# The up products of two MLPs in pairs by Strassen's algorithm, the hidden tensor through DRAM

## The chip, the cores and the metric

The kernel runs on one core of a Trainium2 chip, in one launch. The metric is the device time of that core in microseconds, the median of several runs. TensorE (PE) multiplies, with its weight loads shown as PEld; VectorE (DVE), ScalarE (ACT) and GpSimd (POOL) do the elementwise work; SyncE (SP) issues nearly all DMAs. SBUF is the on-chip memory, PSUM the accumulators that matmuls write.

## The reference

A network of two layers over 16 + 1024 tokens of width 1024, in float32. Each layer adds a mixer (attention and a state space model in layer 0, a gated delta rule in layer 1) and an MLP to the residual, each between two norms. The change is in the MLP alone:

```
def sq_relu_mlp(h, w1, w2):
    return jnp.square(jax.nn.relu(h @ w1)) @ w2
...
hs = hs + rms_norm(sq_relu_mlp(hn, mlp_w1[i], mlp_w2[i]), post_mlp_norm[i])
```

`h` has up to 1040 rows (tokens) of 1024, `w1` is 1024 x 4096 and `w2` 4096 x 1024. In layer 1 the first 16 tokens are not needed any more, so its MLP works on 1024.

## The kernel before

Tokens lie along the free dimension, features in the 128 partitions. A tensor of 1024 features is eight tiles [128, 1040], numbered k; the hidden tensor of 4096 is 32 tiles, numbered m. Tokens go in chunks: `CH` = 352, 344, 344 in layer 0, `CH2` = 344, 344, 336 in layer 1, and `CH3` = 384, 384, 256 for the last product of layer 1.

Every product is made with split operands. A float32 value is held as `hi` (rounded to fp32r) and `lo` (the rest), and `unit` makes three matmuls for each k: hi by hi, hi by lo, lo by hi (lines 174 to 176 of the profile). `weight` makes the halves of a weight tile of [128, 1024]: SP loads `wraw` (two buffers), DVE casts it to `whi` (line 163), POOL subtracts to `wlo` (line 164). `whi` and `wlo` are rings of four tiles, so a cast waits until PE has done with the tile four before it. Each unit (one m, one chunk) goes to one PSUM bank, `mm` with three buffers; `tr` has three more and `ax` two.

`mlp` has two kinds of phases. `up([m])` makes hidden tile m: for each chunk 8 x 3 = 24 matmuls; then `ev` runs DVE (line 384: relu and the factor `rb`, 1/rms per token, from PSUM to a temporary), ACT (line 385: square), and `split`, that is ACT's cast to `hh` (line 226) and DVE's subtraction to `hl` (line 227). `down([a, b])` uses hidden tiles a and b: for each of eight output tiles and each chunk 2 x 3 = 6 matmuls, and DVE adds the bank to `acc` in SBUF (line 408); the first down copies with ACT instead. Group g is the down of hidden tiles 2g and 2g + 1. After four ups in one go the groups follow with two ups between each two of them, one by one, and then comes a last down of four tiles, which also starts the residual and the next norm. The hidden tiles stay in SBUF as `hh` and `hl`, in 33 slots of [128, 1040] that they share with `acc` and others.

The engines take their instructions in order. The Tile framework's scheduler sets each queue's order from its own costs, not from the text's order alone.

Of the kernel before, what the change touches and what calls it, by code (L numbers as in the profile page):

```python
# [1 line left out]

# [24 lines left out]
CH3 = ((16, 384), (400, 384), (784, 256))  # L27

# [20 lines left out]
class Net:  # L49
# [6 lines left out]
    def step(self, strand):  # L56
        """emit the next piece of a strand; whether there was one that need not wait"""
        self.busy, was = True, self.busy
        going = False
        while strand:  # L60
            try:
                going = next(strand[0]) is not WAIT
                break
            except StopIteration:
                strand.pop(0)
        self.busy = was
        return going

    def tick(self, n=1):
        """emit n more pieces of the work that runs beside the present one, of its strands in turn"""  # L70
# [24 lines left out]
    def until(self, name, strand=None):  # L95
        """emit of a strand, or of all, up to what is named"""
        while name not in self.done:
            if strand is None or not self.step(strand):
                self.clock += 0.5
                self.tick()  # L100
# [12 lines left out]
    def pause(self, us):  # L113
        """wait while the tensor engine is given work for some time"""
        t = self.clock + us
        while self.clock < t:
            yield WAIT
# [32 lines left out]
    def weight(self, src, n=1024, spare=False, fast=False):  # L150
        """a weight tile as hi + lo; spare: in slots, beside the weights in use"""
# [15 lines left out]
    def unit(self, pt, kts, wap, rhs, o, n):  # L167
        """One output tile [128, n]: three passes of split products over kts."""
# [25 lines left out]
    def rowscale(self, cols, n, nsub, invd):  # L194
        """cols(j): [128, sub] summands whose sum over partitions is wanted per token; returns
        1/sqrt(sum * invd + eps) in a PSUM tile [128, nsub * sub], the same in every partition."""
# [10 lines left out]
    def spread(self, r, sub, nsub):  # L207
        """[sub, nsub] per-token values to rows that every partition holds."""
# [13 lines left out]
    def split(self, hi, lo, src, gain=None, lo_eng=None):  # L222
        """hi + lo = src (* gain per partition) exactly."""
# [8 lines left out]
    def norm_in(self, st, m, c, chunks, hsn, gcol):  # L232
        """Account one piece of the residual stream for the next product: its square sum, and the
        piece times the norm's gain as hi + lo."""
# [21 lines left out]
    def pieces(self, src, c, chunks, eng, mid=None):  # L256
        """a chunk of a [128, 8, tokens] stream, some feature tiles to a slot"""
# [11 lines left out]
    def first_norm(self):  # L269
        """the first norm, of all but the first chunk in pieces beside the first product"""  # L270
# [29 lines left out]
    def residual(self, acc, ssq, reuse, gpost, hs_old, gpre, chunks):  # L300
        """hs + rms(acc) * gain, and what the next norm or the output takes of it. Returns a hook for
        the last product before it, which goes by chunks of tokens: a chunk is taken up while the next
        one is made. reuse gives its place to the next state."""
# [64 lines left out]

    def mlp(self, layer, st, hs_d, chunks, gpre, ahead=None):
        """gpre: the next norm's gain column, or None at the end."""  # L370
        nc = self.nc
        w1, w2 = self.io["w1"], self.io["w2"]
        hid = {}
        acc = None

        def up(ms, order):
            W = self.w_up if ms[0] == 0 else {m: self.weight(w1[layer, m]) for m in ms}

            def ev(m, c, pt):
                if m not in hid:  # L380
                    hid[m] = (self.slot("hh", F32R), self.slot("hl", F32R))
                o, n = chunks[c]
                t1, t2 = self.tmp("t1"), self.tmp("t2")
                nc.vector.scalar_tensor_tensor(t1[:, :n], pt, 0.0, st["rb"][:, o:o + n], op0=ALU.max, op1=ALU.mult)  # L384
                nc.scalar.activation(t2[:, :n], t1[:, :n], AF.Square)  # L385
                self.split(hid[m][0][:, o:o + n], hid[m][1][:, o:o + n], t2[:, :n])

            self.gemm(ms, range(8), lambda m, k: tuple(w[:, k * 128:(k + 1) * 128] for w in W[m]), lambda k: (st["hi"][k], st["lo"][k]), chunks, order, ev)

        def down(ks, last=False):  # L390
            first = ks[0] == 0
            W = {k: self.weight(w2[layer, k]) for k in ks}
            out, hook, ch = None, None, chunks
            if last:
                if ahead is None:
# [21 lines left out]
        up([0, 1, 2, 3], "c")  # L417
        acc = [self.slot("acc") for _ in range(8)]
        down([0, 1])
        up([4], "m")  # L420
        for g in range(1, 14):
            if g > 1:
                up([2 * g + 2], "m")
            down([2 * g, 2 * g + 1])
            up([2 * g + 3], "m")
        up([30], "m")
        up([31], "m")
        return down([28, 29, 30, 31], True)

# [20 lines left out]
    def s5_params(self):  # L450
# [24 lines left out]
        # powers 0..8 of exp(lambda dt), [128, 9, 16]  # L475
# [17 lines left out]
        # decay of a chunk and its rotation, as unit vectors 1, 2, 4 .. 128 chunks on  # L493
# [14 lines left out]
        # coef = (abar - 1) / lambda  # L508
# [15 lines left out]
        # bbar over b, -c_re and -c_im beside c  # L524
# [17 lines left out]
        # rotation tables over chunks, pairs 0..7 and 8..15  # L542
# [30 lines left out]
    def s5_mats(self, q):  # L573
        """Matrices of the groups 8 q .. 8 q + 7 for chunks of 8 tokens: inputs to state, inputs to
        outputs, and the state before the chunk to outputs."""
# [34 lines left out]
        # impulse response, then the Toeplitz matrices by reading it at shifted places  # L610
# [22 lines left out]
    def s5_ready(self, ud):  # L633
        """what the quarters need, back on chip, a quarter ahead"""
# [30 lines left out]
    def s5_quarter(self, q, ud):  # L665
# [21 lines left out]
        def rotate(dst, src, sign):  # L687
            """dst = src * exp(sign i phi)"""
# [59 lines left out]
    def glu(self):  # L748
        """gelu(y) * sigmoid(gelu(y) w + b), in place, with its square sum"""
# [34 lines left out]
    def normed(self, tiles, ssq, gcol, reuse=None):  # L784
        """rms norm over the features of 4 tiles, as hi + lo"""
# [11 lines left out]
    def attention(self, qd, kd, vd, vd0):  # L797
        """stick-breaking attention, by pairs of heads (a tile of features) and pairs of query tiles"""
# [12 lines left out]
        def load_v(p):  # L811
# [5 lines left out]
            # for a head and a block of keys, hi beside lo  # L817
# [10 lines left out]
        def weights(qk, h, i, kp=None, sg=None):  # L828
            """[q, keys] weights of q tile i"""
# [30 lines left out]
        def later(item, depth=DEP):  # L860
            """products wait for their operands behind the transposes of the next groups"""
# [4 lines left out]
        def outputs(p, pr, h, w, V, osb):  # L866
            # blocks of keys: (index, first q column, q columns)
# [87 lines left out]
    def mixer0(self, st, rows):  # L955
# [3 lines left out]
        # s5 inputs  # L959
# [22 lines left out]
        # token-wise scales for the products that have tokens in the partitions  # L982
# [7 lines left out]
        # values, tokens in the partitions  # L990
# [55 lines left out]
    def out_block(self, acc, w, ks, rhs, first, chunks, W=()):  # L1046
        """products of some feature tiles with the mixer's last weights"""
# [20 lines left out]
    def out_last(self, acc, W, ks, rhs, chunks, gpost, hs_d, gpre, ahead):  # L1068
        """the last of them, and the residual stream after it"""
# [19 lines left out]
    def token_col(self, pt, cols):  # L1089
        """cols(i): summands [128, tokens of tile i]; their sums per token, in column i of pt"""  # L1090
# [3 lines left out]
    def gates(self, st, rc):  # L1094
        """decays and write strengths of all heads, tokens in the partitions: [128, 9, 8]"""
# [74 lines left out]
    def take(self, t):  # L1170
        """weights of one tile of the input projection; loads those of the next one ahead"""
# [6 lines left out]
    def conv_in(self, st, tiles, order, hook=None):  # L1178
        """inputs of the causal convolution, for some tiles of 128 features"""
# [39 lines left out]
    def decays(self, Hs):  # L1219
        """decays between the tokens of a chunk, of all heads"""  # L1220
# [15 lines left out]
    def keys(self, h, xk, H):  # L1236
        """what the chunks of a head need of its keys, short of the state"""
# [66 lines left out]
    def queries(self, h, xq, H):  # L1304
        """what the chunks of a head need of its queries"""
# [34 lines left out]
    def solve(self, n, size, N, U, v):  # L1340
        """U = (I - N)^-1 of n strictly upper triangular blocks, a block in each partition"""
# [28 lines left out]
    def solve_first(self):  # L1370
        """the same for the first tokens of all heads"""
# [12 lines left out]
    def combine(self, H):  # L1384
        """inverses of the 128 x 128 blocks from those of their 32 x 32 blocks"""
# [51 lines left out]
    def values(self, h, x, H):  # L1437
        """values of a head, tokens in the partitions, times the keys' norms"""
# [560 lines left out]
```

## Time and profile before

| what | us |
|---|---|
| three runs | 3014.28, 3022.55, 3031.21 |
| median | 3022.55 |
| profiled execution: its span | 3011.3 |
| PE busy in it | 2838.4 (94%) |
| DVE, ACT, POOL busy in it | 1773.1, 892.8, 864.6 |
| MLP of layer 0, from about 738 to 1460 | 722 |
| MLP of layer 1, from about 2296 to 3000 | 704 |

For the profiled execution the span is the only time at hand. Its rows give a line of the kernel, an engine, an operation with its output and inputs, shapes, a count, the busy time, and the mean of one in ns; behind the second bar stand the engine's idle time ahead of these instructions and what ended it. A matmul's own duration is modelled and overlaps the next; what a matmul costs is read from start to start, or from the number of matmuls in a window.

### The profile page before, as it was taken

To read this page: it belongs to the slowest core of one execution; us is meant where nothing else is said; L and a number is where in the kernel's file an instruction comes from. 1 tells how busy PE (TensorE), PEld (TensorE's weight loads), DVE (VectorE), ACT (ScalarE), POOL (GpSimd) and SP (SyncE) were. 2 spreads that over 40 slices of the span, in tenths; PEclk is the share of its full clock that TensorE was granted. 3 is DMA by queue.
4 is the path that set the end of the run, shared out by engine and by line. 5 is a ranking of instruction groups with operands and counts; after the bars stand their busy time and mean duration, and the time that the engine had idled before them with its cause. 6 is when DMAs were issued, how large, how long until landed. Compare 5 with 4: busy or idle time off the path is not lost. (4 is left out here: it accounts for less than half of the span.)

```text
span 3011.3 us, 44561 instructions
## 1 busy us (share of the span) xinstructions
PE 2838.4 (94%) x17628; PEld 2685.8 (89%) x17628; DVE 1773.1 (59%) x3158; ACT 892.8 (30%) x1934; POOL 864.6 (29%) x628
## 2 busy tenths in 40 slices
PE   7899998999999999999896978999989999999998
PEld 7688667888999999999886978899988999999997
DVE  8633778667455555555646995545546455555555
ACT  4112566554311101111435423334434111111112
POOL 5551225225311221222522132211143222122123
PEclk9989567889999999999998999999999999999999
DMA  3435212134111111111426666453332111111113
GB/s 126 158 127 161 71 43 92 41 104 146 58 50 43 50 46 46 50 42 51 130 85 201 220 205 208 157 153 110 127 106 84 50 50 43 50 50 43 50 50 112
DMA packets 168289, 284.92 MB, mean 95 GB/s; under 512 B 40880, under 2 KB 108672, under 8 KB 168080
## 3 DMA queue, kind: packets, MB, share of 16 engines
q1 hardware_dynamic: 164192, 277.38, 28.8%
q10 hardware_dynamic: 3888, 4.69, 0.4%
q8 instruction: 139, 2.28, 0.3%
q14 instruction: 70, 0.57, 0.1%
HBM read 204.80 MB, written 77.21 MB: 94 GB/s over the span
## 5 line engine op out<-in xcount | busy, mean ns | idle before, releaser
L174 PE MATMUL mm<-ahi,whi 128*128 128x344 f32 (+2 forms) x2592 | 862.4, 333 | 33.5 <-DVE cx L1189 22.1
L164 POOL TENSOR_TENSOR wlo<-wraw,whi 128x1024 fp32r<-128x1024 f32 x181 | 439.5, 2430 | 1504.1 <-DVE whi L163 1138.1
L176 PE MATMUL mm<-ahi,wlo 128*128 128x344 f32 (+2 forms) x2592 | 844.9, 326 | 1.8 <-DVE wlo L164 1.8
L175 PE MATMUL mm<-hl,whi 128*128 128x344 f32 (+4 forms) x1920 | 619.1, 322 | 0.0
L174 PEld LDWEIGHTS mm<-ahi,whi 128*128 128x128 f32 x2592 | 497.2, 192 | 41.7 <-DVE cx L1189 23.3
L176 PEld LDWEIGHTS mm<-ahi,wlo 128*128 128x128 f32 x2592 | 497.0, 192 | 4.5 <-DVE wlo L164 2.9
L176 PE MATMUL mm<-hh,wlo 128*128 128x344 f32 (+4 forms) x1536 | 492.8, 321 | 2.9 <-POOL wlo L164 2.9
L408 DVE TENSOR_TENSOR acc<-mm,acc 128x344 f32<-128x344 f32 (+4 forms) x672 | 343.9, 515 | 253.4 <-PE mm L176 253.4
L174 PE MATMUL mm<-hh,whi 128*128 128x344 f32 (+4 forms) x1536 | 492.0, 320 | 0.1
L385 ACT ACTIVATE t<-t 128x344 f32<-128x344 f32 (+2 forms) x192 | 94.4, 492 | 1093.7 <-DVE t L384 1093.7
L175 PEld LDWEIGHTS mm<-hl,whi 128*128 128x128 f32 x1920 | 363.8, 189 | 1.3 <-issue 0.6
L175 PE MATMUL mm<-ml,whi 128*128 128x344 f32 (+2 forms) x1056 | 340.1, 322 | 0.7 <-DVE ml L227 0.7
L163 DVE CAST whi<-wraw 128x1024 fp32r<-128x1024 f32 x181 | 180.0, 997 | 196.7 <-PE mm L175 160.6
L176 PEld LDWEIGHTS mm<-hh,wlo 128*128 128x128 f32 x1536 | 289.2, 188 | 3.8 <-POOL wlo L164 3.5
L174 PEld LDWEIGHTS mm<-hh,whi 128*128 128x128 f32 x1536 | 289.5, 188 | 0.9 <-DVE acc L408 0.3
L227 DVE TENSOR_TENSOR hl<-t,hh 128x344 fp32r<-128x344 f32 (+2 forms) x192 | 162.2, 845 | 166.6 <-ACT hh L226 165.5
L175 PE MATMUL mm<-mh,whi 128*128 128x344 f32 (+2 forms) x768 | 246.8, 321 | 0.0
L175 PEld LDWEIGHTS mm<-ml,whi 128*128 128x128 f32 x1056 | 199.7, 189 | 1.1 <-DVE ml L227 1.0
L384 DVE SCALAR_TENSOR_TENSOR t<-mm,rb 128x344 f32<-128x344 f32 (+2 forms) x192 | 98.5, 513 | 121.0 <-PE mm L176 121.0
L175 PEld LDWEIGHTS mm<-mh,whi 128*128 128x128 f32 x768 | 144.6, 188 | 0.5 <-issue 0.2
L175 PE MATMUL mm<-hh,whi 128*128 128x344 f32 (+2 forms) x384 | 126.7, 330 | 0.0
L853 DVE TENSOR_TENSOR_SCAN keep<-keep,cst 128x400 f32<-128x400 f32 (+5 forms) x72 | 95.5, 1338 | 45.8 <-ACT keep L851 45.4
(425 smaller groups left out, 4530.0 us busy)
## 6 DMA issues: line engine op xcount, KB each, us to landing
wraw<-w SPq DMA_DIRECT2D x128, 512.0 KB, 3.5
wraw<-wino SPq DMA_DIRECT2D x32, 512.0 KB, 3.7
dm<-dmd SPq DMA_DIRECT2D x16, 520.0 KB, 4.8
hsd<-hs SPq DMA_DIRECT2D x48, 172.0 KB, 1.8
wraw<-wine SPq DMA_DIRECT2D x12, 512.0 KB, 3.7
wraw<-qkd SPq DMA_DIRECT2D x8, 520.0 KB, 3.6
acc<-acc SPq DMA_DIRECT2D x8, 520.0 KB, 4.6
dmd<-grow SPq DMA_DIRECT2D x8, 520.0 KB, 5.3
```

The lines of the kernel that those rows point to most:

```text
L163: nc.vector.tensor_copy(hi[:, :n], raw[:, :n])
L164: (nc.vector if fast else nc.gpsimd).tensor_sub(lo[:, :n], raw[:, :n], f(hi[:, :n]))
L174: nc.tensor.matmul(pt, wh, h[:, o:o + n], start=i == 0, stop=False)
L175: nc.tensor.matmul(pt, wh, l[:, o:o + n], start=False, stop=False)
L176: nc.tensor.matmul(pt, wl, h[:, o:o + n], start=False, stop=i == len(kts) - 1)
L227: (lo_eng or nc.vector).tensor_sub(lo, src, f(hi))
L384: nc.vector.scalar_tensor_tensor(t1[:, :n], pt, 0.0, st["rb"][:, o:o + n], op0=ALU.max, op1=ALU.mult)
L385: nc.scalar.activation(t2[:, :n], t1[:, :n], AF.Square)
L408: nc.vector.tensor_add(acc[m][:, o:o + n], pt, acc[m][:, o:o + n])
L853: v.tensor_tensor_scan(kp[:n, 0:L][:, ::-1], kp[:n, 0:L][:, ::-1], self.one_row[:n, :L], 1.0, op0=ALU.mult, op1=ALU.mult)
```

## The change

The order becomes: ups 0 to 5 as before, then 13 pairs of ups (m = 6 to 31), then 14 downs in a row, then the last down. A pair takes two weight tiles `ra` and `rb` (for m and m + 1) as blocks A11, A12 (k below 4, and from 4) and A21, A22, and the normed input as blocks B11, B12, B21, B22 by k and by token half (520 tokens in layer 0, 512 in layer 1). Strassen's algorithm in Winograd's form makes the four output blocks from seven products of blocks instead of eight, with sums of blocks ahead and behind:

- `halves_T`, once in each MLP, makes the sums of B blocks (T1 to T4) from the residual in DRAM times the norm's gains, and splits them: per layer 8 subtractions on DVE and 8 on POOL, 16 casts on ACT and 16 subtractions on DVE, of 520 or 512 columns, with 16 loads and 16 scalings.
- `ops` makes seven weight operands for each pair: four sums on POOL (`sS`), seven casts on ACT, seven subtractions on POOL, each of 512 columns. An operand takes half a tile of the `whi` and `wlo` rings.
- `product` makes 4 x 3 matmuls for each chunk: two chunks of 260 tokens in layer 0, one of 512 in layer 1. So a pair has 168 matmuls in layer 0 and 84 in layer 1. The banks go round over `mm`, `tr` and one `ax`, seven in all.
- Behind a pair's chunk stand one copy on ACT, seven sums on DVE (one input in PSUM), four `block`s on DVE (relu and `rb`, SBUF alone), and in `put` four squares on ACT and four stores to DRAM (`hd`).

Every hidden tile goes to DRAM, the first six too. `hidden` loads a tile back into a slot (`hr`) and splits it, an ACT cast and a DVE subtraction (line 229 of the changed kernel) of 1040 or 1024 columns. In layer 1 the 14 downs take two chunks of 512 (`CH4`) instead of three. Line numbers of `weight` and `ev` become 165, 166 and 552.

The diff, cut to `mlp` and what it uses; the rest of it removes comments only:

```diff
@@ -25,6 +26,7 @@
 CH3 = ((16, 384), (400, 384), (784, 256))
+CH4 = ((16, 512), (528, 512))
...
@@ -366,32 +368,174 @@
     def mlp_ahead(self, layer):
         self.w_up = {m: self.weight(self.io["w1"][layer, m], fast=FA >> m & 1) for m in range(4)}
+    def halves_T(self, st, hs_d, t0, h, gcol):
+        nc = self.nc
+        T = []
+        for j in range(4):
+            if j < 3:
+                p, q = self.slot("ta"), self.slot("tb")
+                parts = [p[:, :h], p[:, h:2 * h], q[:, :h], q[:, h:2 * h]]
+            else:
+                parts = [self.sp.tile([128, 520], F32, tag="sS", name="sS", bufs=4)[:, :h] for _ in range(4)]
+            for i, x in enumerate(parts):
+                k, o = j + i // 2 * 4, t0 + i % 2 * h
+                nc.sync.dma_start(x, hs_d[:, k, o:o + h])
+                nc.scalar.activation(x, x, AF.Copy, scale=self.gains[:, gcol + k:gcol + k + 1])
+            pl, pr, ql, qr = parts
+            nc.vector.tensor_sub(pl, pr, pl)
+            nc.gpsimd.tensor_sub(pr, qr, pr)
+            nc.vector.tensor_sub(qr, qr, pl)
+            nc.gpsimd.tensor_sub(ql, ql, qr)
+            out = []
+            for x in (parts[:2], parts[2:]):
+                hi, lo = self.slot("th", F32R), self.slot("tl", F32R)
+                for i in range(2):
+                    self.split(hi[:, i * h:i * h + h], lo[:, i * h:i * h + h], x[i])
+                out.append((hi, lo))
+            T.append(out)
+        return T
     def mlp(self, layer, st, hs_d, chunks, gpre, ahead=None):
         nc = self.nc
         w1, w2 = self.io["w1"], self.io["w2"]
+        hd = self.dr.tile([128, 32, NT], F32, tag="hd%d" % layer, name="hd", bufs=1)
         hid = {}
-        acc = None
+        t0, h = (0, 520) if layer == 0 else (16, 512)
+        half = ((0, 260), (260, 260)) if layer == 0 else ((0, 512),)
+        wide = chunks if layer == 0 else CH4
+        def put(m, o, n, x):
+            nc.scalar.activation(x[:, :n], x[:, :n], AF.Square)
+            nc.sync.dma_start(hd[:, m, o:o + n], x[:, :n])
         def up(ms, order):
             W = self.w_up if ms[0] == 0 else {m: self.weight(w1[layer, m]) for m in ms}
             def ev(m, c, pt):
-                if m not in hid:
-                    hid[m] = (self.slot("hh", F32R), self.slot("hl", F32R))
                 o, n = chunks[c]
-                t1, t2 = self.tmp("t1"), self.tmp("t2")
+                t1 = self.tmp("t1")
                 nc.vector.scalar_tensor_tensor(t1[:, :n], pt, 0.0, st["rb"][:, o:o + n], op0=ALU.max, op1=ALU.mult)
-                nc.scalar.activation(t2[:, :n], t1[:, :n], AF.Square)
-                self.split(hid[m][0][:, o:o + n], hid[m][1][:, o:o + n], t2[:, :n])
+                put(m, o, n, t1)
             self.gemm(ms, range(8), lambda m, k: tuple(w[:, k * 128:(k + 1) * 128] for w in W[m]), lambda k: (st["hi"][k], st["lo"][k]), chunks, order, ev)
+        room = []
+        bank = cycle((self.mm, self.tr, self.mm, self.tr, self.mm, self.tr, self.ax))
+        def operand(src, own=False):
+            if not room:
+                hi = self.sb.tile([128, 1024], F32R, tag="whi", name="whi", bufs=4)
+                lo = self.sb.tile([128, 1024], F32R, tag="wlo", name="wlo", bufs=4)
+                room.extend([(hi[:, :512], lo[:, :512]), (hi[:, 512:], lo[:, 512:])])
+            hi, lo = room.pop(0)
+            nc.scalar.copy(hi, src)
+            nc.gpsimd.tensor_sub(lo, src, f(hi))
+            return hi, lo
+        def ops(ma, mb):
+            ra, rb = self.raw(), self.raw()
+            nc.sync.dma_start(ra[:, :1024], w1[layer, ma])
+            nc.sync.dma_start(rb[:, :1024], w1[layer, mb])
+            a11, a12, a21, a22 = ra[:, :512], ra[:, 512:1024], rb[:, :512], rb[:, 512:1024]
+            S = [self.sp.tile([128, 520], F32, tag="sS", name="sS", bufs=4)[:, :512] for _ in range(4)]
+            o = [operand(a11)]
+            nc.gpsimd.tensor_add(S[0], a21, a22)
+            nc.gpsimd.tensor_sub(S[1], S[0], a11)
+            o.append(operand(S[1]))
+            o.append(operand(a12))
+            nc.gpsimd.tensor_sub(S[2], a11, a21)
+            o.append(operand(S[2]))
+            o.append(operand(a22))
+            o.append(operand(S[0]))
+            nc.gpsimd.tensor_sub(S[3], a12, S[1])
+            o.append(operand(S[3]))
+            return o
+        def pair(ma, mb, T):
+            A11, S2, A12, S3, A22, S1, S4 = ops(ma, mb)
+            B11 = lambda k: (st["hi"][k][:, t0:t0 + h], st["lo"][k][:, t0:t0 + h])
+            B21 = lambda k: (st["hi"][k + 4][:, t0:t0 + h], st["lo"][k + 4][:, t0:t0 + h])
+            B22 = lambda k: (st["hi"][k + 4][:, t0 + h:t0 + 2 * h], st["lo"][k + 4][:, t0 + h:t0 + 2 * h])
+            T1, T3 = (lambda k: tuple(x[:, :h] for x in T[k][0])), (lambda k: tuple(x[:, h:2 * h] for x in T[k][0]))
+            T4, T2 = (lambda k: tuple(x[:, :h] for x in T[k][1])), (lambda k: tuple(x[:, h:2 * h] for x in T[k][1]))
+            def product(A, B, then):
+                for c, (o, n) in enumerate(half):
+                    pt = next(bank)()[:, :n]
+                    for i in range(4):
+                        wh, wl = (w[:, i * 128:(i + 1) * 128] for w in A)
+                        bh, bl = B(i)
+                        nc.tensor.matmul(pt, wh, bh[:, o:o + n], start=i == 0, stop=False)
+                        nc.tensor.matmul(pt, wh, bl[:, o:o + n], start=False, stop=False)
+                        nc.tensor.matmul(pt, wl, bh[:, o:o + n], start=False, stop=i == 3)
+                    then(c, o, n, pt)
+            P, U, R, Q = {}, {}, {}, {}
+            def total(x, name, n, *ab):
+                x = self.tmp(name) if x is None else x
+                nc.vector.tensor_add(x[:, :n], *ab)
+                return x
+            def block(m, o, n, x):
+                nc.vector.scalar_tensor_tensor(x[:, :n], x[:, :n], 0.0, st["rb"][:, o:o + n], op0=ALU.max, op1=ALU.mult)
+                put(m, o, n, x)
+            def p1(c, o, n, pt):
+                P[c] = self.tmp("p1")
+                nc.scalar.copy(P[c][:, :n], pt)
+            def p2(c, o, n, pt):
+                block(ma, t0 + o, n, total(P[c], "", n, pt, P[c][:, :n]))
+            def p6(c, o, n, pt):
+                U[c] = total(None, "u2", n, pt, P[c][:, :n])
+            def p7(c, o, n, pt):
+                R[c] = total(None, "u3", n, pt, U[c][:, :n])
+            def p4(c, o, n, pt):
+                block(mb, t0 + o, n, total(None, "c21", n, pt, R[c][:, :n]))
+            def p5(c, o, n, pt):
+                Q[c] = total(U[c], "", n, pt, U[c][:, :n])
+                block(mb, t0 + h + o, n, total(R[c], "", n, pt, R[c][:, :n]))
+            def p3(c, o, n, pt):
+                block(ma, t0 + h + o, n, total(Q[c], "", n, pt, Q[c][:, :n]))
+            product(A11, B11, p1)
+            product(S2, T2, p6)
+            product(A12, B21, p2)
+            product(S3, T3, p7)
+            product(A22, T4, p4)
+            product(S1, T1, p5)
+            product(S4, B22, p3)
+        def hidden(k):
+            raw = self.slot("hr")
+            hi, lo = self.slot("hh", F32R), self.slot("hl", F32R)
+            nc.sync.dma_start(raw[:, t0:NT], hd[:, k, t0:NT])
+            self.split(hi[:, t0:NT], lo[:, t0:NT], raw[:, t0:NT])
+            hid[k] = (hi, lo)
         def down(ks, last=False):
             first = ks[0] == 0
+            for k in ks:
+                hidden(k)
             W = {k: self.weight(w2[layer, k]) for k in ks}
-            out, hook, ch = None, None, chunks
+            out, hook, ch = None, None, wide
             if last:
+                ch = chunks
                 if ahead is None:
                     ch = CH3
                 if ahead is not None:
@@ -415,19 +559,17 @@
             return out
         up([0, 1, 2, 3], "c")
+        T = self.halves_T(st, hs_d, t0, h, G_PREMLP + 8 * layer)
+        for m in range(4, UPC):
+            up([m], "m")
+        for m in range(UPC, 32, 2):
+            pair(m, m + 1, T)
         acc = [self.slot("acc") for _ in range(8)]
-        down([0, 1])
-        up([4], "m")
-        for g in range(1, 14):
-            if g > 1:
-                up([2 * g + 2], "m")
+        for g in range(14):
             down([2 * g, 2 * g + 1])
-            up([2 * g + 3], "m")
-        up([30], "m")
-        up([31], "m")
         return down([28, 29, 30, 31], True)
...
-NSLOT, NTMP, AHEAD = 33, 10, 4
+NSLOT, NTMP, AHEAD, UPC = 33, 10, 4, 6
...
-    st, hs = N.mlp(0, st, hs, CH, G_PREMIX + 8, N.mixer1_ahead)
+    with N.tc.tile_pool(name="m0", bufs=1) as N.sp:
+        st, hs = N.mlp(0, st, hs, CH, G_PREMIX + 8, N.mixer1_ahead)
...
-    N.mlp(1, st, hs, CH2, None)
+    with N.tc.tile_pool(name="m1", bufs=1) as N.sp:
+        N.mlp(1, st, hs, CH2, None)

```

How instructions move, first on DVE in layer 0, between two groups. `acc` is the accumulation, `whi` a weight tile's cast, `t` an up's evacuation, `hl` a hidden tile's subtraction. Before:

```order
L408 TENSOR_TENSOR acc<-mm,acc 128x352
L408 TENSOR_TENSOR acc<-mm,acc 128x344
L163 CAST whi<-wraw 128x1024
L408 TENSOR_TENSOR acc<-mm,acc 128x344
L163 CAST whi<-wraw 128x1024
L384 SCALAR_TENSOR_TENSOR t_9937<-mm,rb 128x352
L227 TENSOR_TENSOR hl<-t_9938,hh 128x352
```

Now:

```order
L165 CAST whi<-wraw 128x1024
L552 TENSOR_TENSOR acc<-mm,acc 128x344
L165 CAST whi<-wraw 128x1024
L552 TENSOR_TENSOR acc<-mm,acc 128x352
L229 TENSOR_TENSOR hl<-hr,hh 128x1040
L552 TENSOR_TENSOR acc<-mm,acc 128x344 x2
```

The two casts and a whole tile's `hl` subtraction now stand between the accumulations of one group and of the next, with no up behind them. This form stands at 8 of the 14 boundaries behind the downs of layer 0; at one there is an accumulation more ahead of `hl`, the last four have no `hl` left, and the first has both casts and then two `hl` in a row.

Then DVE in layer 1, at the same kind of place. Before:

```order
L408 TENSOR_TENSOR acc<-mm,acc 128x344 x2
L163 CAST whi<-wraw 128x1024
L408 TENSOR_TENSOR acc<-mm,acc 128x336
L163 CAST whi<-wraw 128x1024
L384 SCALAR_TENSOR_TENSOR t_26732<-mm,rb 128x344
L227 TENSOR_TENSOR hl<-t_26733,hh 128x344
```

Now:

```order
L552 TENSOR_TENSOR acc<-mm,acc 128x512 x9
L165 CAST whi<-wraw 128x1024 x2
L552 TENSOR_TENSOR acc<-mm,acc 128x512
L229 TENSOR_TENSOR hl<-hr,hh 128x1024
L552 TENSOR_TENSOR acc<-mm,acc 128x512 x6
```

Both casts now stand together, and `hl` follows one accumulation later; seven boundaries of layer 1 have this form.

Last POOL, which before had in these phases `L164 TENSOR_TENSOR wlo<-wraw,whi 128x1024` alone, one for each weight tile. Now, between two pairs of layer 0 (`sS` is a sum of weight blocks, `wlo` the low half of an operand):

```order
L438 TENSOR_TENSOR wlo<-wraw,whi 128x512
L449 TENSOR_TENSOR sS<-wraw 128x512
L450 TENSOR_TENSOR sS<-sS,wraw 128x512
L438 TENSOR_TENSOR wlo<-sS,whi 128x512
L453 TENSOR_TENSOR sS<-wraw 128x512
L438 TENSOR_TENSOR wlo<-sS,whi 128x512
L457 TENSOR_TENSOR sS<-wraw,sS 128x512
```

Sums and subtractions of 512 columns alternate on POOL, eleven of them for each pair.

More of the change, by code (lines that the diff above doesn't have):

```diff
@@ L1 @@
 import math
+from itertools import cycle
 import numpy as np
```

## The prediction

> **What bounds the kernel now.** I read the page first (busy shares, then the groups), then windows of the two MLPs, then the timeline around the places that the new order touches. The page's first rows:
>
> ```profile
> span 3011.3 us, 44561 instructions
> PE 2838.4 (94%) x17628; PEld 2685.8 (89%) x17628; DVE 1773.1 (59%) x3158; ACT 892.8 (30%) x1934; POOL 864.6 (29%) x628
> ```
>
> TensorE leads. Windows inside the MLP of layer 0 and of layer 1 (columns: sum, then PE, PEld, DVE, ACT, POOL, granted clock, DMA share, GB/s):
>
> ```profile
> 900.00:1000.00 100.00, 100.00 (x633) 100.00 (x632) 53.08 (x86) 13.71 (x29) 21.62 (x9) 1.00 0.15 48
> 2500.00:2600.00 100.00, 100.00 (x643) 100.00 (x642) 55.16 (x93) 11.62 (x24) 20.00 (x9) 1.00 0.14 43
> ```
>
> PE is never idle there, at full clock: a matmul costs 100/633 = 0.158 us in layer 0 and 100/643 = 0.1555 in layer 1. So fewer or cheaper matmuls pay in full, and every new PE wait costs in full.
>
> **Matmuls removed.** The pairs run at 260 and 512 columns. Prices by start to start: 256 columns (end of the last down of layer 1, first and last of 14), 512 columns (attention values, first and last of 14):
>
> ```profile
> 2984.36 0.28 PE L174 MATMUL mm<-hh,whi 128*128 128x256 f32 x1
> ...
> 2985.89 0.28 PE L175 MATMUL mm<-hl,whi 128*128 128x256 f32 x1
> ```
> ```profile
> 91.00 0.39 PE L1003 MATMUL mm<-wlo,ahi 128*16 128x512 f32 x1
> ...
> 94.01 0.40 PE L1004 MATMUL mm<-whi,alo 128*128 128x512 f32 x1
> ```
>
> 1.53/13 = 0.1177 us and 3.01/13 = 0.2315 us: 0.00044 us a column, so 0.1195 at 260 (estimate). Layer 0: 26 up products of 8 x 3 x 3 = 72 matmuls are 1872 x 0.158 = 295.8 us; 13 pairs of 7 x 2 x 12 = 168 are 2184 x 0.1195 = 261.0: -34.8. Layer 1: 1872 x 0.1555 = 291.1 against 13 x 84 = 1092 x 0.2315 = 252.8: -38.3. Layer 1's 14 downs go from 2016 matmuls (313.5 us) to 1344 of 512 (311.1): -2.4. Together **-75.5 us**.
>
> **The pairs' other work.** Rows for weights, sums and casts (groups; the POOL ones at 512 columns by form):
>
> ```profile
> L164 POOL TENSOR_TENSOR wlo<-wraw,whi 128x1024 fp32r<-128x1024 f32 x181 | 439.5, 2430 | 1504.1 <-DVE whi L163 1138.1
> L408 DVE TENSOR_TENSOR acc<-mm,acc 128x344 f32<-128x344 f32 (+4 forms) x672 | 343.9, 515 | 253.4 <-PE mm L176 253.4
> L163 DVE CAST whi<-wraw 128x1024 fp32r<-128x1024 f32 x181 | 180.0, 997 | 196.7 <-PE mm L175 160.6
> ```
> ```profile
> L591 POOL TENSOR_TENSOR s5mo<-s5mo,s5c 128x512 f32<-128x512 f32 x8 | 12.0, 1504 | 0.2
> L591 POOL TENSOR_TENSOR s5mi<-s5mi,s5c 128x512 f32<-128x512 f32 x8 | 10.1, 1282 | 0.1
> ```
>
> A pair gives PE 168 x 0.1195 = 20.1 us (layer 1: 84 x 0.2315 = 19.4). POOL gets 11 operations of 512: between 11 x 2.43/2 = 13.4 and 11 x 1.50 = 16.5. DVE gets 14 sums and 8 blocks of 260, at most 22 x 0.515 = 11.3; the blocks read SBUF alone and may hold POOL up (below), 8 x 0.5 = 4 at most. So POOL needs 13.4 to 20.5 of 20.1; I take 17.4 (middle row, 1.28 x 11 = 14.1, with 0.4 for a 260-wide block). Eight half tiles hold operands six products ahead (17 us), and seven PSUM banks absorb late sums. **Cost 0**, cover 2.0 to 2.7 us a pair. ACT's casts and squares lie ahead of need in the same way.
>
> The hidden tensor's way through DRAM adds 32 x 0.53 MB out and in to each layer, some 48 GB/s over 700 us, as much again as the windows show (share 0.15 to about 0.3). All of it is issued on SP, in order with the weight loads, and a store there waits for its square. Landing times now (KB, median us):
>
> ```profile
> wraw<-w SPq DMA_DIRECT2D x128, 512.0 KB, 3.5
> hsd<-hs SPq DMA_DIRECT2D x48, 172.0 KB, 1.8
> ```
>
> A pair's weights are asked for about one pair (20 us) before use and a hidden row some 20 us or more before its down; 5 us of landing and a queued store are covered: cost 0, and up to 1 us a pair, 26, if a store held up a weight load; that end lies inside rival (c).
>
> The T operands of each layer (16 tiles) are built beside up[4] and up[5], 2 x 72 x 0.158 = 22.8 us. DVE has 24 subtractions of 520 on SBUF alone there, each half of this row's 1.22, so 14.6 us, beside two weight casts and 6 evacuations:
>
> ```profile
> L227 DVE TENSOR_TENSOR qkl<-wraw,qkh x8: 1216/1232/3067, 277.5 to 510.3; 128x1040 fp32r<-128x1040 f32 x8
> ```
>
> They come in bursts ahead of evacuations, with POOL's 8 between; bounds 0 and 4 us a layer, I take 2: **+4**.
>
> **The downs follow one another.** Before, every change from a down to the next weights falls in front of an up, whose units are 24 matmuls (3.8 us). The timeline at such a place, DVE and POOL, then PE:
>
> ```profile
> 846.49 0.69 DVE L163 CAST whi<-wraw 128x1024 fp32r<-128x1024 f32 x1
> 847.09 0.51 DVE L408 TENSOR_TENSOR acc<-mm,acc 128x344 f32<-128x344 f32 x1
> 847.51 2.73 DVE L163 CAST whi<-wraw 128x1024 fp32r<-128x1024 f32 x1
> 850.86 0.53 DVE L384 SCALAR_TENSOR_TENSOR t<-mm,rb 128x352 f32<-128x352 f32 x1 [0.62 <-PE mm L176]
> ```
> ```profile
> 847.30 2.38 POOL L164 TENSOR_TENSOR wlo<-wraw,whi 128x1024 fp32r<-128x1024 f32 x1 [19.96 <-DVE whi L163]
> 850.37 2.40 POOL L164 TENSOR_TENSOR wlo<-wraw,whi 128x1024 fp32r<-128x1024 f32 x1 [0.68 <-issue]
> ```
> ```profile
> 846.80 0.32 PE L174 MATMUL mm<-ahi,whi 128*128 128x352 f32 x1
> ```
>
> The second cast takes 2.73 us for 0.69: it ends 0.56 after POOL's subtraction (849.68). The accumulation at 847.09 (one input in PSUM) is not held up though POOL starts meanwhile. So a DVE operation on SBUF alone waits out a running POOL tensor_tensor, and all behind it on DVE wait too. Here that is free: the next evacuation is due at 850.86.
>
> After, the next group's accumulations stand behind it, one per 6 matmuls = 0.95 us in layer 0, with three PSUM banks. Take T0 as the first matmul of the next group (846.80 above). Order cast, acc, cast, acc, hl, acc: the second cast ends T0+3.4, first accumulation +3.9; POOL's second subtraction runs +3.6 to +6.0; hl (1040 columns on SBUF, 1.22 alone) ends about +7.1; second accumulation +7.6. PE's fourth unit is due at +2.85 and waits for the first bank to +3.95 (1.1 us); the fifth is then due at +4.9 and waits to +7.55 (2.65).
>
> That is 3.75 us, at 8 places of layer 0; one place with a further accumulation ahead of hl 3.3; three without hl 1.1 each. The first boundary casts twice and then makes both hl that its own products need: second hl behind the second subtraction at about +7, less 0.6 of work available: 6.4. The last group waits for two subtractions in a row, 2.8 more than now. Sum **+45.8**. In layer 1 a unit is 6 x 0.2315 = 1.39 us and mostly both casts stand together, so the second runs unhindered, as here:
>
> ```profile
> 812.20 1.30 DVE L163 CAST whi<-wraw 128x1024 fp32r<-128x1024 f32 x2 [18.88 <-PE mm L175]
> ...
> 813.03 5.09 POOL L164 TENSOR_TENSOR wlo<-wraw,whi 128x1024 fp32r<-128x1024 f32 x2 [20.08 <-DVE whi L163]
> ```
>
> hl waits only the first subtraction, to about T0+4.1, and the fourth unit, due at 4.17, waits 0.6: 7 x 0.6, one of the long kind 1.9, first boundary 6.1, last 2.9: **+15.1**. Bounds for these stalls: 0 (hl gets through ahead of POOL) and twice, 122, if accumulations were held too, which 847.09 speaks against.
>
> **The clock.** Windows of 3.4 us (PE busy with matmuls started, granted clock, DMA share, GB/s), each followed by the next:
>
> ```profile
> 170.40:173.80 3.40, 1.16 (x7) 1.00 0.05 17
> 173.80:177.20 3.40, 0.88 (x3) 0.51 0.02 7
> ...
> 2293.50:2296.90 3.40, 1.06 (x11) 1.00 0.15 51
> 2296.90:2300.30 3.40, 3.40 (x12) 0.51 0.00 0
> 1829.30:1832.70 3.40, 1.67 (x15) 1.00 1.01 351
> 1832.70:1836.10 3.40, 3.40 (x31) 1.00 0.71 271
> ```
>
> With 7 or 11 matmuls in a window the next runs at half clock, with 15 it does not. A window that holds a 2.65 us stall has 0.75 us = 5 matmuls. By where the window falls I give that two chances in three; half clock for 3.4 us costs 1.7 less the waiting in it, about 1.4: 1.0 for each of 9 places, 2 for each first boundary: **+13**; bounds 0 and 26. The Trainium skill, TensorE: Matmul & The Clock Gate, section "HAM oscillation", asks only that PE gaps stay under about 3.4 us; by it a 2.65 us stall leaves the clock alone and the sum is 13 us less.
>
> **Sum.** -75.5 + 4 + 45.8 + 15.1 + 13 = **+2.4 us**. The profiled execution's span of 3011.3 would be 3013.7; it lies 11.2 under the median of the runs, 3022.55, so **3025 us**, about no change (from no change a measurement tells 0.5%, 15 us).
>
> **Rivals.**
> (a) The boundaries stay hidden: POOL lets hl through, or its second subtraction comes after. For it: layer 1's order already does so for the cast. Against: 847.51 waited to POOL's end. -75.5 + 4: 2951 us.
> (b) The stalls come but no half clock: 1829.30 with 15 matmuls speaks for it, 2293.50 with 11 against. 3012 us. The skill's rule named above would give this.
> (c) The pairs are bound by POOL: decided where its 11 subtractions and sums, with DVE's blocks in between, exceed 20.1 us (19.4 in layer 1). For it: 1.50 a piece plus 4 is 20.5, and each waits for an ACT cast. At 1.5 us over in 26 pairs: +39, 3064 us. Against: 1.28 and 1.21 rows.
> (d) 260-column matmuls cost no less than 344-column ones, held by their weight loads:
>
> ```profile
> L174 PEld LDWEIGHTS mm<-hh,whi 128*128 128x128 f32 x1536 | 289.5, 188 | 0.9 <-DVE acc L408 0.3
> ```
>
> Then layer 0 gains nothing and loses 2184 x 0.158 - 295.8 = 49 instead, 3109 us. 256 columns at 0.1177 speak against it.
>
> **How the numbers follow.** My forecast 0.47, its own range 3005 to 3050 (stalls 10 us less, clock at 26, T at 8); (a) 0.15, (b) 0.12, (c) 0.23, (d) 0.03. Faster than 3007: (a), a third of (b) and a sixth of the forecast: 0.27. Within: 0.37 (most of the forecast, half of (b)). Slower than 3038: (c), (d), a fifth of the forecast: 0.36. Range 2955 to 3087: from just inside (a) to beyond (c), which also takes in doubled stalls (3025 + 61 = 3086).
>
> **What would show it.** Windows in the pairs: PE at 100 of 100, about 837 matmuls in 100 us in layer 0, 432 in layer 1; under 800 and 415 speak for (c), with POOL near 100. In layer 0's downs: PE idle ended by DVE's acc, 3.7 us at each boundary, hl lasting over 3 us behind POOL's wlo, granted clock under 1. PE at 100 there is (a). A gap between up[5] and the first pair over 4 us breaks the T term.

## The result, and the profile after

The changed kernel takes 3065.18 us (median of 4 runs, 3058.10 to 3069.21) against 3022.36; the ratio is 1.0147, 95% interval 1.0118 to 1.0177. It is slower by 1.2 to 1.8%: 40 us above the forecast of 3025 and above the forecast's own range, 3005 to 3050, but inside the whole range given, 2955 to 3087. Of the profiled execution, the page's first rows:

```profile
span 3067.2 us, 43940 instructions
PE 2816.3 (92%) x16488; PEld 2534.5 (83%) x16488; DVE 1894.7 (62%) x3195; ACT 1020.7 (33%) x2084; POOL 1165.8 (38%) x878
```

PE has 1140 instructions fewer and is busy for 22 us less, yet the span is longer: PE waits. Windows by phase tell where (PE busy with its matmuls, granted clock, DMA share, GB/s), for each layer the ups 4 and 5 with the T operands, the pairs, and the downs:

```profile
769.00:819.70 50.70, 43.39 (x263) 0.97 0.39 123
819.70:1081.20 261.50, 261.50 (x2186) 1.00 0.35 107
1081.20:1492.20 411.00, 366.90 (x2126) 0.93 0.26 89
2353.40:2401.90 48.50, 43.07 (x260) 0.93 0.40 127
2402.00:2655.90 253.90, 253.90 (x1094) 1.00 0.33 111
2656.00:3023.00 367.00, 341.07 (x1454) 0.98 0.28 96
```

The pairs run without a gap at full clock, 261.5 and 253.9 us where the prediction had 261.0 and 252.8. Layer 0's downs take 411 us. Their matmuls are worth 318.5 us at before's price, and before's last down took 19.8 up to the residual, so 72.7 us are lost there; in layer 1 it is 367.0 less 311.1 and 20.9, that is 35. The T phases lose 50.7 - 263 x 0.158 = 9.1 us and 48.5 - 260 x 0.1555 = 8.1. Between the same marks in both traces (from the end of the mixer's residual to that of the MLP) layer 0's MLP is 45.2 us longer and layer 1's 0.5 us shorter: 44.7, which agrees with the medians' 42.8. The spans differ by 55.9, since layer 1's mixer, which the change leaves alone, took 837.7 us here and 825.2 in the one traced execution of before; in the nine experiments it took 831 to 842, also with layer 0's MLP as before, and before's traced execution was 11 us under its own median. That points to chance; it was not tested further.

A boundary between two groups of layer 0, on the timeline of DVE, then POOL and PE:

```profile
1196.92 0.68 DVE L165 CAST whi<-wraw 128x1024 fp32r<-128x1024 f32 x1
1197.52 0.51 DVE L552 TENSOR_TENSOR acc<-mm,acc 128x344 f32<-128x344 f32 x1
1197.94 2.74 DVE L165 CAST whi<-wraw 128x1024 fp32r<-128x1024 f32 x1
1200.60 0.51 DVE L552 TENSOR_TENSOR acc<-mm,acc 128x352 f32<-128x352 f32 x1
1201.04 3.23 DVE L229 TENSOR_TENSOR hl<-hr,hh 128x1040 fp32r<-128x1040 f32 x1
```
```profile
1197.73 2.40 POOL L166 TENSOR_TENSOR wlo<-wraw,whi 128x1024 fp32r<-128x1024 f32 x1 [19.34 <-DVE whi L165]
1200.81 2.36 POOL L166 TENSOR_TENSOR wlo<-wraw,whi 128x1024 fp32r<-128x1024 f32 x1 [0.68 <-PE mm L178]
```
```profile
1201.17 0.43 PE L176 MATMUL mm<-hh,whi 128*128 128x352 f32 x1 [0.91 <-DVE acc L552]
1204.75 0.42 PE L176 MATMUL mm<-hh,whi 128*128 128x344 f32 x1 [2.35 <-DVE acc L552]
```

The second cast ends 0.55 us after POOL's first subtraction, `hl` 1.1 us after the second, and PE waits twice for `acc`, 0.91 and 2.35 us where 1.1 and 2.65 had been worked out. What follows, in three windows of 3.41 us:

```profile
1199.07:1202.48 3.41, 2.42 (x14) 1.00 0.38 117
1202.48:1205.89 3.41, 1.14 (x7) 1.00 0.60 179
1205.89:1209.30 3.41, 3.41 (x14) 0.50 0.82 329
```

After the window with 7 matmuls PE goes at half clock for a whole window. By the granted clock of the trace sixteen such windows lie in the 411 us, which is 27 us of full clock, lost in part while PE waits anyway.

### The profile page after: what moved, and what is told of

Its sections match the earlier page's. It is cut to its first block, busy times and chain, and to the rows that moved or that the text cites. A ratio compares the mean times of both kernels' runs of the same rounds, so it can differ in the third digit from the quotient of the medians.

```text
span 3067.2 us, 43940 instructions
## 1 busy us (share of the span) xinstructions
PE 2816.3 (92%) x16488; PEld 2534.5 (83%) x16488; DVE 1894.7 (62%) x3195; ACT 1020.7 (33%) x2084; POOL 1165.8 (38%) x878
## 5 line engine op out<-in xcount | busy, mean ns | idle before, releaser
L176 PE MATMUL mm<-hh,whi 128*128 128x512 f32 (+4 forms) x1312 | 469.6, 359 | 61.7 <-DVE acc L552 45.4
L176 PE MATMUL mm<-ahi,whi 128*128 128x344 f32 (+2 forms) x1344 | 470.0, 350 | 57.4 <-DVE cx L1331 30.1
L178 PE MATMUL mm<-hh,wlo 128*128 128x512 f32 (+4 forms) x1312 | 465.2, 355 | 5.4 <-POOL wlo L166 5.4
L552 DVE TENSOR_TENSOR acc<-mm,acc 128x352 f32<-128x352 f32 (+4 forms) x568 | 321.9, 578 | 229.2 <-PE mm L178 229.0
L178 PE MATMUL mm<-ahi,wlo 128*128 128x344 f32 (+2 forms) x1344 | 449.7, 335 | 2.2 <-DVE wlo L166 2.2
L176 PEld LDWEIGHTS mm<-ahi,whi 128*128 128x128 f32 x1344 | 265.8, 198 | 67.7 <-DVE cx L1331 31.5
L178 PEld LDWEIGHTS mm<-ahi,wlo 128*128 128x128 f32 x1344 | 265.0, 197 | 5.2 <-DVE wlo L166 3.4
L438 POOL TENSOR_TENSOR wlo<-sS,whi 128x512 fp32r<-128x512 f32 x104 | 143.1, 1379 | 30.9 <-ACT whi L437 30.8
L177 PE MATMUL mm<-ml,whi 128*128 128x344 f32 (+2 forms) x432 | 140.9, 326 | 0.7 <-DVE ml L229 0.7
L229 DVE TENSOR_TENSOR hl<-hr,hh 128x1040 fp32r<-128x1040 f32 (+1 forms) x64 | 113.9, 1780 | 40.8 <-ACT hh L228 40.8
```

The source lines that it names most:

```text
L176: nc.tensor.matmul(pt, wh, h[:, o:o + n], start=i == 0, stop=False)
L177: nc.tensor.matmul(pt, wh, l[:, o:o + n], start=False, stop=False)
L178: nc.tensor.matmul(pt, wl, h[:, o:o + n], start=False, stop=i == len(kts) - 1)
L229: (lo_eng or nc.vector).tensor_sub(lo, src, f(hi))
L438: nc.gpsimd.tensor_sub(lo, src, f(hi))
L552: nc.vector.tensor_add(acc[m][:, o:o + n], pt, acc[m][:, o:o + n])
```

## The experiments

Theory A: DVE waits out POOL's subtraction, the accumulations queue behind, three banks fill, PE waits and its clock falls. It was tried from three sides: more banks, no POOL work, shorter POOL work. Each ratio is to the kernel before, measured again beside the experiment (medians 3020.83 to 3022.46); what is saved or gained is counted from the changed kernel's 3065.18.

**Six banks in the downs.**

```diff
-            pt = self.mm()
+            pt = (bank or self.mm)()      # downs but the last: mm and tr in turn
```

> The downs (all but the last of each layer) take their PSUM banks in turn from mm and tr, six instead of three; nothing else changes. Theory A (DVE waits out POOL's subtraction at each boundary, and PE waits for DVE only because three banks run full): with six banks the wait at a boundary of layer 0 falls from 3.6 us to about 0.9 (unit 7 due at 6.65, first bank of the second accumulation free at 7.55), at those without hl from 1.1 to 0, in layer 1 to 0, and the half clock behind it goes. Saved: 9 x 2.7 + 3 x 1.1 + 9 of clock in layer 0, some 13 in layer 1, together about 50 us: 3015 us. Rival B (PE waits at these places for weights or hidden rows, not for banks): no change, 3065.

Measured: 2993.94 us, ratio to before 0.9904 (0.9879 to 0.9928). PE in layer 0's downs by windows; then its waits there (us in all, times, longest) in the changed kernel; then, in this run, its wait for `acc` and DVE's `hl` and casts:

```profile
1088.20:1450.10 361.90, 345.33 (x2126) 0.99 0.29 101
```
```profile
PE mm L176 <- DVE acc L552: 31.4, 21, 2.4
PE mm L176 <- ACT hh L228: 3.9, 2, 2.4
PE mm L176 <- ACT acc L550: 3.7, 2, 2.3
PE mm L178 <- POOL wlo L166: 2.6, 2, 1.4
PE mm L177 <- DVE hl L229: 1.9, 1, 1.9
```
```profile
PE tr L176 <- DVE acc L553: 5.7, 8, 0.7
```
```profile
L229 DVE TENSOR_TENSOR hl<-hr,hh 128x1040 fp32r<-128x1040 f32 x30 | 56.4, 1879 | 18.6 <-ACT hh L228 18.6
L165 DVE CAST whi<-wraw 128x1024 fp32r<-128x1024 f32 x31 | 47.9, 1547 | 18.2 <-PE tr L177 18.2
```

DVE and POOL do the same work, and DVE still waits for POOL as long as in the changed kernel (56.0 and 47.8 us, shown below), yet 49 of 411 us are gone. So these are waits for banks, and rival B is out. The saving, 71 us, is 21 more than forecast, since the clock stays at 0.99, and layer 1's downs save 22 and not 13.

**The downs' wlo on DVE**, so that POOL has nothing to do there.

```diff
-            W = {k: self.weight(w2[layer, k]) for k in ks}
+            W = {k: self.weight(w2[layer, k], lo_eng=None if last else nc.vector) for k in ks}
```

> The wlo subtractions of the downs' weights move from POOL to DVE, so POOL does nothing in the downs. Theory A (the port that DVE waits for): the casts take 0.69 and hl 1.22 again; DVE has 5.1 us of SBUF work per group with accumulations in between, each wait under the two units of slack: waits in layer 0 fall from 3.6 to under 1 us a boundary, about 45 us less with the clock, 3020. Rival C (DVE is simply too full in the downs): 2 x 1.23 us more on DVE per group make it worse, 28 x 2.5 us at most, over 3065.

Measured: 2986.12 us, ratio 0.9878 (0.9851 to 0.9904). DVE's groups in layer 0's downs, of the changed kernel and then here:

```profile
L229 DVE TENSOR_TENSOR hl<-hr,hh 128x1040 fp32r<-128x1040 f32 x30 | 56.0, 1866 | 5.3 <-ACT hh L228 5.3
L165 DVE CAST whi<-wraw 128x1024 fp32r<-128x1024 f32 x31 | 47.8, 1544 | 21.0 <-PE mm L177 21.0
```
```profile
L229 DVE TENSOR_TENSOR hl<-hr,hh 128x1040 fp32r<-128x1040 f32 x30 | 37.0, 1232 | 3.9 <-ACT hh L228 3.9
L166 DVE TENSOR_TENSOR wlo<-wraw,whi 128x1024 fp32r<-128x1024 f32 x26 | 31.5, 1216 | 0.0
L165 DVE CAST whi<-wraw 128x1024 fp32r<-128x1024 f32 x30 | 24.7, 826 | 18.2 <-PE mm L177 18.2
```

DVE gets 31.5 us of work more and the kernel is 79 us faster: the casts and `hl` alone had spent 42 us waiting for POOL. DVE is not too full; rival C is out. It is 34 us more than forecast, of which layer 1's downs, left out of the forecast, make 23 (344.0 us for 367.0). The order shifts too (accumulations between the subtractions), and SP's weight loads no longer wait for POOL, so not all of it is DVE's wait for POOL.

**Halved subtractions on POOL**, DVE's order unchanged.

```diff
-        (nc.vector if fast else nc.gpsimd).tensor_sub(lo[:, :n], raw[:, :n], f(hi[:, :n]))
+        for c in range(cut):              # 2 in the downs but the last
+            s = slice(c * n // cut, (c + 1) * n // cut)
+            (nc.vector if fast else nc.gpsimd).tensor_sub(lo[:, s], raw[:, s], f(hi[:, s]))
```

> Each wlo subtraction of the downs' weights is cut on POOL into two of 512 columns (1.2 us each for 2.4); DVE's order is unchanged. Theory A, with DVE getting in between two POOL operations: the second cast ends at T0+2.3, the first accumulation at 2.8 (in time), hl waits to 3.5 and ends at 4.7, the second accumulation at 5.2, for which the fifth unit waits 1.4 us. A boundary of layer 0 loses 1.4 for 3.6, those without hl nothing, and windows with 1.4 us of waiting keep the clock: 9 x 2.2 + 3 + about 14 less in layer 0, some 4 in layer 1: about 3025 us. If the wait lasts as long as POOL has work queued, whatever its pieces: no change, 3065.

Measured: 3050.60 us, ratio 1.0103 (1.0073 to 1.0134): 15 us gained where 40 were expected. The timeline, DVE, SP and ACT:

```profile
1194.07 1.63 DVE L165 CAST whi<-wraw 128x1024 fp32r<-128x1024 f32 x1
...
1196.06 1.90 DVE L231 TENSOR_TENSOR hl<-hr,hh 128x1040 fp32r<-128x1040 f32 x1
...
1206.79 1.24 DVE L231 TENSOR_TENSOR hl<-hr,hh 128x1040 fp32r<-128x1040 f32 x1 [2.77 <-ACT hh L230]
```
```profile
1196.88 3.83 SPq L156 DMA_DIRECT2D wraw<-w  x2
1200.76 1.33 SPq L529 DMA_DIRECT2D hr<-hd  x2
```
```profile
1205.70 1.06 ACT L230 CAST hh<-hr 128x1040 fp32r<-128x1040 f32 x1 [18.59 <-DMA hr<-hd]
```

(`...` stands for rows left out.) The cast takes 1.63 for 2.74 and `hl` 1.90 for 3.23: DVE does wait for a running piece only, and gets in ahead of the next. But a new wait stands in the middle of the group: `hl` waits 2.77 us for ACT's cast, that for the hidden row, and its load stands on SP behind two weight loads. In layer 1, where 4 us had been expected, halving alone saves nothing: PE's waits in its downs come to 28.5 us for 25.9.

**Hidden rows loaded from ACT's queue**, alone and with the halved subtractions. The same is seen on POOL, SP and DVE of the changed kernel in layer 1, and what PE waits for it:

```profile
2836.15 6.08 POOL L166 TENSOR_TENSOR wlo<-wraw,whi 128x1024 fp32r<-128x1024 f32 x2 [17.88 <-PE mm L178]
```
```profile
2838.91 3.67 SPq L156 DMA_DIRECT2D wraw<-w  x2
2842.64 7.90 SPq L527 DMA_DIRECT2D hr<-hd  x2
```
```profile
2848.96 1.23 DVE L229 TENSOR_TENSOR hl<-hr,hh 128x1024 fp32r<-128x1024 f32 x1 [3.19 <-ACT hh L228]
```
```profile
2850.84 0.51 PE L176 MATMUL mm<-hh,whi 128*128 128x512 f32 x1 [1.66 <-DVE acc L552]
```

SP's second weight load goes out when POOL's second subtraction has ended (2842.23), and the hidden row's load behind it. ACT's cast of this row is put down to PE by the profile and not to the load, so at this one place the cause is not shown; over layer 1's downs the loads end 133.1 of the 209.9 us that ACT idles ahead of these casts. The experiment decides.

```diff
-            nc.sync.dma_start(raw[:, t0:NT], hd[:, k, t0:NT])
+            nc.scalar.dma_start(raw[:, t0:NT], hd[:, k, t0:NT])
```

> The loads of hidden rows (hr) are issued from ACT's queue instead of SP's. Theory D (in layer 1 these loads stand on SP behind weight loads that wait for POOL, so the second hl of a group is late and PE waits 1.0 to 1.8 us a group, and 7 us at the first boundary): layer 1 gains 8 x 1.2 + 7, some 16 us, layer 0 next to nothing: 3049. Rival (they wait for slots, wherever issued): no change, 3065.

Measured: 3050.72 us, ratio 1.0094 (1.0072 to 1.0115), as forecast; the rival is out. PE's waits in layer 1's downs, of the changed kernel and then here:

```profile
PE mm L176 <- DVE acc L552: 13.4, 16, 1.9
PE mm L176 <- ACT hh L228: 8.2, 2, 6.6
```
```profile
PE mm L176 <- DVE acc L552: 8.8, 10, 1.9
PE mm L176 <- ACT hh L228: 3.4, 1, 3.4
```

> Halved wlo subtractions and hr loads from ACT's queue together. Halving alone cut the wait at a boundary of layer 0 from 3.6 to 1.2 us, but a new one of about 2 us came in the middle of each group, where hl waits for hr. Theory D (SP's order): it goes, with its half clock, 8 x 2 + 8 in layer 0, and 12 us in layer 1 as with hr on ACT alone: 3050 - 36 = 3015 us. If hr is late because DRAM or slots are: the gain is that of hr on ACT alone, 15 us: 3035.

Measured: 2996.46 us, ratio 0.9922 (0.9895 to 0.9949), 19 us better than the theory asked. Alone the two gain 15 and 14 us, together 69: each hid the other's wait. PE's waits for `acc` in layer 0's downs are down to 8.0 us in 8 waits, the longest 1.0.

**Six banks in up[4] and up[5]**, beside the T operands. The waits of PE in that phase of the changed kernel, and DVE ahead of the longest:

```profile
PE mm L176 <- DVE t L422: 7.3, 2, 5.4
```
```profile
798.67 0.69 DVE L229 TENSOR_TENSOR tl<-ta,th 128x520 fp32r<-128x520 f32 x1
799.49 2.42 DVE L229 TENSOR_TENSOR tl<-tb,th 128x520 fp32r<-128x520 f32 x2
801.83 4.66 DVE L229 TENSOR_TENSOR tl<-sS,th 128x520 fp32r<-128x520 f32 x4
806.42 1.36 DVE L422 SCALAR_TENSOR_TENSOR t<-mm,rb 128x352 f32<-128x352 f32 x3
```

Seven subtractions stand between two evacuations, 7.7 us.

```diff
-            self.gemm(..., chunks, order, ev)
+            self.gemm(..., chunks, order, ev, None, None if order == "c" else lambda: next(six)())
```

> Only up[4] and up[5], beside which the T operands are built, take six banks (mm and tr) instead of three. Theory E (their evacuations stand on DVE behind up to 7.7 us of T subtractions, and PE waits for a bank): the waits of 2.2 and 5.7 us in layer 0 and the like in layer 1, with the half clock behind them, go: about 9 us a layer, 3047 us. Rival (the first pair's second product then waits for T itself): the wait only moves, 3060 or more.

Measured: 3051.71 us, ratio 1.0104 (1.0078 to 1.0131), 13 us less where 18 were expected. PE has no wait for DVE in this phase any more; by the phases layer 0 loses 9 us less there and layer 1 7. The pair's second product does not wait for T.

**One layer alone**, with before's `mlp` as `mlp_old`.

```diff
-        st, hs = N.mlp(0, st, hs, CH, G_PREMIX + 8, N.mixer1_ahead)
+        st, hs = N.mlp_old(0, st, hs, CH, G_PREMIX + 8, N.mixer1_ahead)
```

> Layer 0's MLP is that of the kernel before, layer 1's the changed one. By the two traces layer 0 lost 45 us and layer 1 about 1 us, the mixer between them about 11: 3023 if the 11 comes with layer 0's MLP or is chance, 3034 if it belongs to the mixer. Rival (layer 1 carries the loss): over 3050.

Measured: 3015.63 us, ratio 0.9987 (0.9971 to 1.0003). It is 7 us below the lower of the two figures; the rival is out. Layer 0 carries the loss; layer 1 comes out about even.

**The order without the algorithm.**

```diff
-NSLOT, NTMP, AHEAD, UPC = 33, 10, 4, 6
+NSLOT, NTMP, AHEAD, UPC = 33, 10, 4, 32
-        T = self.halves_T(st, hs_d, t0, h, G_PREMLP + 8 * layer)
```

> The changed order without the algorithm: all 32 ups as plain products in one row, no T operands, hidden through DRAM, the downs in a row (layer 1's at 512). The pairs' gain goes (34.8 + 37 us more), the T phases' loss too (about 17 less): 3065 + 72 - 17 = 3120 us, if the pairs run at the price of their columns and the downs lose what they lost. If the downs' loss came from the pairs' leftover work: under 3080.

Measured: 3105.53 us, ratio 1.0287 (1.0260 to 1.0313). Layer 0's downs by windows:

```profile
1098.50:1502.70 404.20, 362.88 (x2126) 0.94 0.25 86
```

The downs lose nearly what they lose behind the pairs (404 us for 411; the step from pairs to downs, below, is absent here), and PE waits for `acc` the same 31.4 us in 21 waits. So the loss belongs to the order of the phases, not to the algorithm: that order, with the hidden tensor's way through DRAM that goes with it, costs 83 us alone; the two were not parted. Against it the pairs with their T phases are worth 40 us. It was 15 us less than expected.

**All remedies**, the four edits above: six banks in the downs and in ups 4 and 5, the downs' wlo on DVE, hidden rows from ACT's queue.

> Together: six banks in the downs and in up[4] and up[5], the downs' wlo on DVE, hr loads on ACT's queue. From 2986 us with the wlo on DVE alone: 18 for the T phases, about 5 in layer 0's downs and 6 in layer 1's: 2957 us. If the three remedies cure the same waits, nothing is added: 2980 or more.

Measured: 2966.96 us, ratio 0.9823 (0.9789 to 0.9856): faster than both kernels, 55 us under before. Downs of layer 0 and 1 by windows:

```profile
1080.40:1429.30 348.90, 342.87 (x2126) 0.99 0.33 103
2586.40:2928.40 342.00, 335.27 (x1454) 0.99 0.33 103
```

Both lie 10 to 11 us over the price of their matmuls. It is 19 us better than the downs' wlo on DVE alone, not 29: the remedies for the downs overlap, while that for the T phases comes on top.

## Why the prediction was right or wrong

- **The number.** About no change was forecast, and the change costs 43 us. The stated range holds the measured time only because its upper end was set by rival (c) and by doubled stalls, and neither came: that is luck. Layer 0's downs lost 72.7 us where 56.8 had been put (45.8 and 11 of the clock), layer 1's 35 where 17.1 had (15.1 and 2), the T phases 17.2 where 4 had.
- **The matmuls' price** held: 261.5 and 253.9 us for 261.0 and 252.8. **The pairs' other work** was hidden as said; rival (c) gave the time nearest the measured one, 3064, for a reason that is not there: PE never waits in the pairs, and POOL is busy for 180.7 us of layer 0's 261.5. Rival (d) falls with the same rows.
- **The boundary** held in place, order and size: 0.91 + 2.35 us for 1.1 + 2.65, and three experiments show its parts. All PE's waits in layer 0's downs come to 31.4 + 3.9 + 3.7 + 2.6 + 1.9 and a last 0.2, 43.7 us; without the 3.7 of the step from pairs to downs (below), which the sum did not hold, that is 40.0 where 45.8 had been put.
- **The clock** is the term of the sum that was mis-sized most: 13 us, with 26 as its end. PE is busy for 366.9 us in layer 0's downs whose matmuls are worth 338.3 (318.5 and 19.8), so half clock cost 28.6 us there, which with the 43.7 of waits makes up the 72.7. In layer 1 it cost 9.1 (341.1 for 332.0). In layer 0 nine of the ten boundaries with `hl` are followed by half clock, not two in three, some for two or three windows. The Trainium skill's rule (TensorE: Matmul & The Clock Gate, section "HAM oscillation"), no PE gaps over about 3.4 us, is not enough here: no wait in layer 0's downs is over 2.5 us. In the windows above a gap of 2.35 us, nearly alone in its window, was followed by half clock; in layer 1 one wait of 1.95 us left 1.46 us of matmuls in the window from 2718.00 to 2721.41, and the next went at 0.50.
- **The hidden rows at cost 0, "covered"**, is the step whose mechanism failed. They were asked for late, behind weight loads that wait on SP for POOL's subtraction. PE's waits in layer 1's downs came to 25.9 us where 15.1 had been put: 1.66 inside the group shown, and at the first boundary 1.6 + 1.3 + 6.6 where 6.1 had been put for `hl` alone. Loads from ACT's queue gave 12 us of layer 1's downs back (355.3 us for 367.0), with the halved subtractions 23 (343.7). Layer 0 hid it behind the wait at the boundary until that was cut.
- **The T phases**, 2 us a layer, cost 9.1 and 8.1; even the end given, 4, was too low. The count of DVE's work was right, but not the wait of three banks behind seven subtractions in a row.
- **From pairs to downs** no term stood. The first down's copies on ACT queue behind a square that waits for DVE, which waits for POOL; of two waits, 3.7 us, the longer:

```profile
1086.60 0.66 PE L176 MATMUL mm<-hh,whi 128*128 128x352 f32 x1 [2.35 <-ACT acc L550]
```

## What to carry to other kernels

A phase can be the cover of another: what a change of order moves away from a long-running neighbour has to be priced again, in time that PE's banks can bridge. With three banks that is two units, 1.9 us in layer 0, less the accumulation's 0.5; with six the waits for `acc` fell from 31.4 us to 5.7. Before taking an algorithm for slower, give its evacuations more banks and take from the queue whatever makes it wait. Waits in series hide each other: two remedies of 15 us each gave 69 together.

## What the runs showed of the hardware

A DVE cast or subtraction on SBUF waits only for the POOL operation that runs, not for POOL's queue: with pieces of half the size the cast took 1.63 us for 2.74. POOL seems to wait in turn: two subtractions that take 2.40 us where DVE leaves them alone took 6.08 together beside a cast and an `hl`. And one PE wait of 2.35 us, nearly alone in a window of 3.41 us, was followed by 3.41 us at half clock; in layer 1 one of 1.95 us was.
